# One inference step of a hybrid decoder on one core: sample chain between dense matmuls, gate sums normed earlier, parked sums added later

## The chip, the core and the metric

The kernel runs on one core of a Trainium2 chip. Its engines are TensorE (PE: matmuls; PEld: its weight loads), VectorE (DVE), ScalarE (ACT), GpSimd (POOL) and SyncE (SP). SP only issues transfers; ACT and POOL issue some beside their other work. The metric is the time of one execution on the device in microseconds, as the median of several runs. A profiled execution gives a trace with the start, length and releaser of every instruction.

## The reference

One layer for 512 prompt tokens and for 8 sequences of 4 sample tokens, in float32:

```python
h = h + 0.5 * rmsnorm(swiglu(rmsnorm(h, norm_g[0]), wg[0], wu[0], wd[0]), norm_g[1])
m, c_kv, k_r, s_fin = mixer(rmsnorm(h, norm_g[2]), ...)
h = h + rmsnorm(m, norm_g[3])
h = h + 0.5 * rmsnorm(swiglu(rmsnorm(h, norm_g[4]), wg[1], wu[1], wd[1]), norm_g[5])
def swiglu(x, wg, wu, wd):
    return (jax.nn.silu(x @ wg) * (x @ wu)) @ wd
```

The width is 1024, the inner width of both FFNs 2816. The mixer has four heads of a gated linear recurrence (HGRN2) and four heads of latent attention; the sample tokens attend to 4096 cached positions, which lie in pages of 128 rows and are found through a page table. Eight results are returned, the two token outputs, new cache rows and the recurrent states.

## The kernel before, in words

All activations lie transposed: the model width on the partitions (8 tiles of 128), the 544 tokens along the free axis. `prompt[0]` and `prompt[1]` are two halves of 256 prompt tokens, and `TP:` are the 32 sample columns, so a half with its share of sample columns, `even[x]`, is W2 = 272 wide. A matmul in float32 precision is made of three of reduced precision: `split` casts a high part on ScalarE (L158, L195, L219) and takes the rest on VectorE (L159, L196, L220), and the products high-high, low-high and high-low are added in one accumulator.

The stages follow one another on TensorE: the first FFN (`ffn0`), the mixer's projections and recurrence, the attention of the prompt, the decode of the sample, the sample chain, the second FFN (`ffn1`) and its end.

*Projection.* `project(x)` computes the attention output of half x times w_o: 8 columns `d`, each from a 512 KB load `wraw<-w_o` (L218), a cast (L219), a subtraction (L220) and 24 matmuls (L246). `weight` gives each column one of NW = 2 pairs of buffers `wh` and `wl`. Behind each column stand a copy (L680), a square (L267) and a scaling (L270) on ScalarE. The old activations `h[x]` of both halves are loaded (L671) into the same tile `q0`, so the load of half 1 comes after half 0 is done with it. `squares(0)` then squares the eight tiles of half 0 at once (L708), and `root` makes the norm of it.

*Decode.* `decode()` yields once per step of a tick. POOL gathers pages, VectorE turns 32x32 blocks (L1379), TensorE takes scores (L1391) and values (L1424), ScalarE and VectorE do the softmax between. `phase_a()` is a second generator, `gb`: project(1), then the gate, up and down columns of the first FA = 8 tiles of the second FFN. Its matmuls over 512 columns are the filler of the decode. The loop at L1604 decides how many filler steps follow one tick: `PRE` for the first ten ticks, one afterwards. `decode_new()` computes the scores of the four new tokens of each sequence and goes with the early odd ticks.

*Sample chain.* `decode_end()` merges the decode's parts, projects them by w_o for the 32 sample columns (`rowprod`, L1492, into `sr`), turns the result (`back`, L1498, into `tp`), and takes two column sums over partitions (`colsum`, L1507, into `pr`: eight matmuls with a matrix of ones per sum). Each sum gives a norm (`rstd`, L185). Only then can the sample columns of the second FFN's input be split, since `ffn1` takes 272 columns at a time with sample columns among them. After each yield of this chain two filler steps are taken, as long as there are some.

*Second FFN.* `ffn1` goes through pairs of tiles j = 4 to 10; j = 4 by `classic`, the others by `seven`, a seven-product scheme with banks X, Y, Z (L447). In each j, `tile_pair` with w_g makes G, then with w_u makes V; `gated(H, *late, i)` of the j before stands in between and multiplies G by the norm r4 (L526), takes the sigmoid (L289 to L291: exponential, plus one, reciprocal) and multiplies (L528, L529). In `seven`, L478 to L484 prepare the weight sums, and `plus` (L496) reads a bank so that it comes free. `fill` puts down-projection matmuls (L228, into `dn`) between the products, `PACE` of them at a time, from the list `downs`. The sums of down projections lie parked in DRAM: mA[0] and mA[1] from the decode's filler, mA[2] from `park` in j = 6. At j = 7 the first two are fetched into mT (L1738: a plain copy by SP, then an accumulating transfer by POOL), at j = 8 all of `downs` is done at once and mA[2] is added by two accumulating transfers (L1743).

*The end.* `lastdown` multiplies the last six tiles by w_d and adds the result to mT, output tiles 0 and 1 first, then 2, then 3 to 7; `Finish` norms and writes.

Within an engine's queue the program order is what the builder makes of the order of the code: `tc.issue_after(mark[0])` lets an instruction stand behind a marked one, and a tile of a pool with N buffers makes the writer wait for the readers of the tile N before.

## Time and profile before

| what | us |
|---|---|
| median of 3 runs (1255.78 to 1258.1) | 1257.3 |
| the profiled execution | 1267.38 |
| its span, first to last instruction | 1265.6 |
| TensorE busy | 1223.2 (97%) |
| VectorE busy | 981.6 (78%) |
| ScalarE busy | 703.3 (56%) |
| POOL busy | 91.2 (7%) |
| mean granted TensorE clock | 0.988 |

Times in the trace are counted from the start of the span. The first FFN lies before about 375, the mixer up to 575, the prompt's attention up to 701, project(1) between 701 and 730, the decode up to about 974, the sample chain from 974 to 994, `ffn1` up to about 1225. In a row of the timeline the bracket at the end tells how long the engine stood idle before the instruction, and what ended it. In a row of equal windows, the busy times are given with the number of instructions behind them. L numbers are lines of the kernel before.

### The profile page before, as it was taken

How to read it: one execution, taken by the hardware profiler on the slowest of the kernel's cores; microseconds unless marked ns; L12 is line 12 of the kernel's file. 1: busy time of each engine (PE TensorE's matmuls, PEld its weight loads, DVE VectorE, ACT ScalarE, POOL GpSimd, SP SyncE). 2: the span in 40 equal slices, each digit the busy share in tenths (PEclk: the TensorE clock that was granted, in tenths of full speed). 3: DMA queues.
4: the chain of work that ended last, by engine and by line, in shares of the span. 5: the costliest groups of instructions: out<-in, count | busy, mean ns of one | idle time of the engine just before them, and what ended most of it. 6: DMA issues, size and time to landing. Idle time of an engine off the chain costs nothing.

```text
span 1265.6 us, 29473 instructions
## 1 busy us (share of the span) xinstructions
PE 1223.2 (97%) x12244; PEld 1122.7 (89%) x12244; DVE 981.6 (78%) x1992; ACT 703.3 (56%) x1524; POOL 91.2 (7%) x102
## 2 busy tenths in 40 slices
PE   8999999999999999999999899999999999999997
PEld 7999999999999988989989777667677999999997
DVE  7897778888678887777886778878885759768765
ACT  7675545454566644545677655545455346554363
POOL 0000000000000000000000212332321000000000
PEclk9999999999999999999999899999999899999999
DMA  6233323332165221333325765688568467764231
GB/s 234 84 117 100 99 86 100 101 100 80 52 224 165 67 87 65 92 88 128 114 73 150 268 235 191 218 300 304 201 233 294 148 256 239 172 180 119 80 109 71
DMA packets 82070, 190.70 MB, mean 151 GB/s; under 512 B 14032, under 2 KB 39664, under 8 KB 77456
## 3 DMA queue, kind: packets, MB, share of 16 engines
q1 hardware_dynamic: 60208, 117.60, 28.7%
q0 software_dynamic: 15840, 63.58, 15.5%
q10 hardware_dynamic: 5888, 7.65, 1.8%
q8 instruction: 96, 1.57, 0.5%
q14 instruction: 38, 0.31, 0.1%
HBM read 172.63 MB, written 16.16 MB: 149 GB/s over the span
## 4 chain that ended last, share of the span: by engine, by line
PE 79%; DVE 10%; ACT 5%; DMA 4%; issue 2%; SPq 0%; DVEq 0%; ACTq 0%
PE acc L246 19%; PE acc L228 11%; PE dn L228 10%; PE Y L447 8%; PE Z L447 6%; PE X L447 5%; PE s L1391 3%; PE acc L627 3%; PE acc L1800 2%; PE o L1424 2%; DVE kh L1379 1%; DMA wraw<-w_u 1%; PE pa L957 1%; DMA wraw<-w_g 1%; ACT pbuf L1415 1%
## 5 line engine op out<-in xcount | busy, mean ns | idle before, releaser
L246 PE MATMUL acc<-uh,wh 128*128 128x272 f32 (+2 forms) x496 | 161.1, 325 | 0.7 <-ACT uh L195 0.7
L246 PE MATMUL acc<-ul,wh 128*128 128x272 f32 (+2 forms) x496 | 155.7, 315 | 0.7 <-DVE ul L196 0.7
L246 PE MATMUL acc<-uh,wl 128*128 128x272 f32 (+2 forms) x496 | 155.3, 314 | 0.5 <-DVE wl L220 0.5
L220 DVE TENSOR_TENSOR wl<-wraw,wh 128x1024 fp32r<-128x1024 f32 (+2 forms) x80 | 86.2, 1078 | 35.8 <-ACT wh L219 33.4
L219 ACT CAST wh<-wraw 128x1024 fp32r<-128x1024 f32 (+2 forms) x80 | 74.8, 935 | 67.1 <-PE acc L246 49.3
L228 PE MATMUL dn<-hh,dh 128*128 128x272 f32 x384 | 111.4, 290 | 0.0
L228 PE MATMUL dn<-hh,dl 128*128 128x272 f32 x384 | 110.5, 288 | 0.0
L228 PE MATMUL dn<-hl,dh 128*128 128x272 f32 x384 | 110.5, 288 | 0.0
L246 PEld LDWEIGHTS acc<-uh,wh 128*128 128x128 f32 x496 | 93.2, 188 | 14.1 <-issue 9.1
L246 PEld LDWEIGHTS acc<-uh,wl 128*128 128x128 f32 x496 | 93.1, 188 | 7.0 <-issue 1.3
L246 PEld LDWEIGHTS acc<-ul,wh 128*128 128x128 f32 x496 | 93.3, 188 | 6.2 <-issue 1.2
L228 PEld LDWEIGHTS dn<-hh,dh 128*128 128x128 f32 x384 | 72.3, 188 | 1.0 <-issue 0.2
L228 PEld LDWEIGHTS dn<-hl,dh 128*128 128x128 f32 x384 | 72.5, 189 | 0.0
L228 PEld LDWEIGHTS dn<-hh,dl 128*128 128x128 f32 x384 | 72.1, 188 | 0.0
L158 ACT CAST sh<-wraw 128x512 fp32r<-128x512 f32 (+1 forms) x66 | 40.7, 657 | 44.3 <-PE Z L447 27.3
L158 ACT CAST wh<-wraw 128x512 fp32r<-128x512 f32 (+1 forms) x67 | 41.0, 651 | 39.9 <-PE Z L447 22.5
L1391 PEld LDWEIGHTS s<-kh,q 64*32 64x32 f32 x2560 | 38.6, 105 | 26.5 <-issue 19.1
L1391 PE MATMUL s<-kh,q 64*32 64x128 f32 x2560 | 54.3, 273 | 7.6 <-issue 5.6
L158 ACT CAST dh<-wraw 128x512 fp32r<-128x512 f32 x48 | 29.8, 620 | 48.0 <-PE dn L228 43.6
L159 DVE TENSOR_TENSOR wl<-wraw,wh 128x512 fp32r<-128x512 f32 (+1 forms) x67 | 46.8, 726 | 7.8 <-ACT wh L158 7.2
L1415 ACT COPY pbuf<-pt 32x64 f32<-32x64 f32 x192 | 46.5, 242 | 9.3 <-DVE pt L1411 6.6
L159 DVE TENSOR_TENSOR sl<-wraw,sh 128x512 fp32r<-128x512 f32 (+1 forms) x66 | 46.6, 734 | 3.8 <-ACT sh L158 3.0
(708 smaller groups left out, 4131.1 us busy)
## 6 DMA issues: line engine op xcount, KB each, us to landing
wraw<-w_u SPq DMA_DIRECT2D x44, 512.0 KB
wraw<-w_g SPq DMA_DIRECT2D x43, 512.0 KB
wraw<-w_d SPq DMA_DIRECT2D x24, 512.0 KB
wraw<-w_in SPq DMA_DIRECT2D x24, 512.0 KB
wraw<-w_o SPq DMA_DIRECT2D x16, 512.0 KB
wraw<-w_d SPq DMA_DIRECT2D x16, 384.0 KB
wraw<-w_d SPq DMA_DIRECT2D x16, 256.0 KB
mA<-sit ACTq DMA_DIRECT2D x16, 256.0 KB
```

The source lines that it names most:

```text
L158: nc.scalar.copy(hi, src)
L159: (eng or nc.vector).tensor_tensor(lo, src, f32(hi), op=ALU.subtract)
L219: nc.scalar.copy(wh[:, :kt], w[:, :kt])
L220: nc.vector.tensor_tensor(wl[:, :kt], w[:, :kt], f32(wh[:, :kt]), op=ALU.subtract)
L228: nc.tensor.matmul(out, a, b, start=n == 0, stop=n == last)
L246: nc.tensor.matmul(acc[:, :n], a[:, k], b[:, k], start=k + i == 0, stop=k == kt - 1 and i == 2)
L447: nc.tensor.matmul(bank, a[p][:, k], b[q][:, k], start=first and k + n == 0, stop=k == 3 and n == 2, skip_group_check=True)
L627: nc.tensor.matmul(accs[x, d], wts[d][p][:, k], hs[k // 2][q][:, k % 2, x], start=k + n == 0, stop=k == nf - 1 and n == 2)
L1391: nc.tensor.matmul(self.s[r][c * 32 : c * 32 + 32, :P], q[rs, j], kh, start=st + jj == 0, stop=st == len(JS) - 1 and jj == 1, skip_group_c ...
L1415: (nc.scalar.copy if g else nc.vector.tensor_copy)(self.p[g * 32 : g * 32 + 32, c // 2, c % 2 * 4 : c % 2 * 4 + 4, self.i * 16 : self.i * ...
L1424: nc.tensor.matmul(o[g : g + 32, :R], self.p[:, c, a], self.craw[c][:, a], start=i + c == 0 and a < 4, stop=i + c == 2 and a >= 4, skip_gr ...
L1800: nc.tensor.matmul(accs[x, d], wts[d][p][:, k], hs[k // 2][q][:, k % 2, x], start=k + n == 0, stop=k == nf - 1 and n == 2)
```

## The change

It has five parts.

1. **project(1).** Its `h[1]` gets a slot of its own (`m`), so that the load goes out earlier. `weight` takes a ready pair of buffers by `home`, and every third column of project(1) gets such a pair, called `hl`. `squares` becomes a generator, of which one square follows each step of project(1); `root(0, ..)` comes at step 9 in place of 2. `sil` has one buffer in place of two.
2. **Decode.** `decode_new` starts after tick 12 and has its temporaries in other tiles. The gather slots are in another order, and the third and fourth gather are placed otherwise. The filler goes by `PRE, BODY = 22, 95`: 22 steps over the first 14 ticks, 73 over the next 80. Before it was 22 over 10, and one for each tick after.
3. **Sample chain.** It moves out of `decode_end` into `sample_u`. `decode_end` has 3, 4 and 1 filler steps behind its yields, `sample_u` two behind each. `colsum` is one matmul over 256 columns and a reduction on VectorE. The pools of `ffn1` open before it, and the first weights of w_g are split before it.
4. **Gate sums.** G is multiplied by r4 right after the products that make it, in place of at the head of `gated`, an iteration later.
5. **Parked sums.** `settle(d)` adds four of the eight output tiles of mA[2]: `settle(0)` at j = 10, `settle(4)` after the last `fill`. The `fill(99)` at j = 8 is gone, and all fetches at j = 7 are issued by POOL.

ScalarE, in j = 5 of `ffn1`: `sit` is the sigmoid, `ha` a pair of gate sums, `dh` the high part of a w_d tile for the down projection, `hb<-X` the reader of bank X. Before:

```order
L499 COPY tq<-X 128x272
L289 ACTIVATE sit<-ha 128x544
L290 ACTIVATE sit<-sit,ones 128x544
L158 CAST dh<-wraw 128x512
L291 ACTIVATE sit<-sit 128x544
L158 CAST dh<-wraw 128x512
L505 COPY hb<-X 128x272
```

and now (lines of the changed kernel, where the sigmoid's three are L288 to L290 and the reader of X is L504):

```order
L498 COPY tq<-X 128x272
L288 ACTIVATE sit<-ha 128x544
L289 ACTIVATE sit<-sit,ones 128x544
L290 ACTIVATE sit<-sit 128x544
L158 CAST wh<-S 128x512
L504 COPY hb<-X 128x272
L158 CAST wh<-S 128x512
L158 CAST dh<-wraw 128x512
L158 CAST hh<-ha 128x544
L158 CAST dh<-wraw 128x512
```

Both casts `dh` moved behind the third step of the sigmoid.

TensorE, in the sample chain from the turning of the projected rows (`tp`) to the second column sum (`pr`), before; `acc` are the first products of `ffn1`:

```order
L1498 MATMUL tp<-ident,rs_t 128x128 x2
L1507 MATMUL pr<-s_post,ones 128x32 x8
L228 MATMUL acc<-uh,sh 128x272
L228 MATMUL acc<-ul,sh 128x272
L228 MATMUL acc<-uh,wh 128x272
L1507 MATMUL pr<-s_post,ones 128x32 x8
```

and now, around the first of the two sums, where L1331 is the column sum and the rows L245 are filler:

```order
L245 MATMUL acc<-hh,wh 128x512
L245 MATMUL acc<-hl,wh 128x512
L245 MATMUL acc<-hh,wl 128x512
L1331 MATMUL pr<-s_post,ones 128x256
L245 MATMUL acc<-hh,wh 128x512
L245 MATMUL acc<-hl,wh 128x512
```

Twelve filler matmuls now stand ahead of each step of this chain and twelve more behind the first sum; the second sum stands behind 14 of the products of `ffn1`.

ScalarE, in project(1): the w_o columns are cast in the rows `wh<-wraw` (before) and `hl<-wraw` (the third pair). Before:

```order
L680 COPY hh<-acc 128x256 x2
L267 ACTIVATE ssq<-hh 128x256
L219 CAST wh<-wraw 128x1024
L708 ACTIVATE sq_8792<-q_8242 128x256
L708 ACTIVATE sq_8795<-q_8242 128x256
```

and now, with line numbers of the changed kernel:

```order
L683 COPY hh<-acc 128x256 x2
L266 ACTIVATE ssq<-hh 128x256
L266 ACTIVATE sq_8856<-hh 128x256
L269 ACTIVATE hh<-hh,gv 128x256 x2
L711 ACTIVATE sq_8860<-q_8242 128x256
L218 CAST hl<-wraw 128x1024
```

The cast moved behind a second square, the two scalings and a square of half 0.

The diff, without the unchanged functions that it moves ahead of the decode:

```diff
-PRE = (2, 2, 2, 2, 2, 2, 2, 2, 3, 3)
+PRE, BODY = 22, 95
...
-    def weight(srcs, kt, staged=False):
+    def weight(srcs, kt, staged=False, home=None):
         pool, sfx, bufs = (st, "x", STAG) if staged else (sb, "", NW)
         w = mk([P, 8, P], F32, "wraw", 5, pool=sb)
-        wh = mk([P, 8, P], F32R, "wh" + sfx, bufs, pool=pool)
-        wl = mk([P, 8, P], F32R, "wl" + sfx, bufs, pool=pool)
+        wh, wl = home or [mk([P, 8, P], F32R, n + sfx, bufs, pool=pool) for n in ("wh", "wl")]
...
-    def block_ffn(i, B, r=None):
+    def block_ffn(i, B):
...
         def gated(H, G, V, i):
             z = G[:, 2 * i : 2 * i + 2]
             t = mk([P, 2, W2], F32, "sit", 2)
-            if r is not None:
-                nc.vector.tensor_tensor(z, z, r, op=ALU.mult)
             sigmoid(t, z)
...
     def project(x, o, nxt, pool=None):
-        if not qts:
+        if x:
+            h[x] = actslot("m", 1, n=HS[0])
+        else:
             qts.append(mk([P, 2 * KQ * HS[0]], F32, "q0", pool=dK))
-        h[x] = qts[0][:, : KD * HS[0]].rearrange("p (k t) -> p k t", k=KD)
+            h[x] = qts[0][:, : KD * HS[0]].rearrange("p (k t) -> p k t", k=KD)
         nc.sync.dma_start(h[x], hsp[:, :, prompt[x]])
         yield
         mT = mk([P, KD, HS[0]], F32, "hh", pool=pool) if pool else actslot("m", x, n=HS[0])
         sacc = tmp("ssq", HS[0])
 
         def wo(d):
-            return weight([wcols(w_o, 0, KD, d * P)], KD)
+            home = None
+            if pool and d % 3 == 2:
+                home = mk([P, 2, KD, P], F32R, "hl", pool=pool)
+                home = home[:, 0], home[:, 1]
+            return weight([wcols(w_o, 0, KD, d * P)], KD, home=home)
...
             nc.scalar.activation(q, h[x][:, k], AF.Square)
             if k:
                 nc.vector.tensor_tensor(acc, acc, q, op=ALU.add)
-        return acc
+            yield acc
...
-        acc = squares(0)
         pj = project(1, oo[1], to_ffn, ffa)
         next(pj)
+        sq = squares(0)
         for n, _ in enumerate(pj):
-            if n == 2:
+            acc = next(sq, None) or acc
+            if n == 9:
                 root(0, acc)
...
+    def colsum(q):
+        pr = ps("pr", PRT)[:, : KD * TS]
+        nc.tensor.matmul(pr, ones, q.rearrange("p k t -> p (k t)"), start=True, stop=True)
+        t = mk([P, TS], F32, "tS", 1, pool=sb)
+        nc.vector.tensor_reduce(t, pr.rearrange("p (k t) -> p t k", k=KD), axis=AX.X, op=ALU.add)
+        return t
...
+    def sample_u():
+        hS = srow("ssq")
+        nc.sync.dma_start(hS, hsp[:, :, TP:])
+        tok = tmp("rs_t", 2 * P)
+        for r in range(2):
+            nc.scalar.copy(tok[:, r * P : (r + 1) * P], rowprod(oTs, wo[r]))
+            yield
+        tp = back(tok)
+        yield
+        mS, sq = srow("ssq"), srow("s_post")
+        nc.scalar.activation(sq, tp, AF.Square)
+        nc.vector.tensor_tensor(mS, tp, gains(3), op=ALU.mult)
+        s = mk([P, TS], F32, "sS", 1, pool=sb)
+        rstd(s, colsum(sq), D)
+        yield
+        nc.vector.tensor_tensor(mS, mS, over(s), op=ALU.mult)
+        nc.vector.tensor_tensor(hS, hS, mS, op=ALU.add)
+        nc.sync.dma_start(hs2[:, :, TP:], hS)
+        sq = srow("s_post")
+        nc.scalar.activation(sq, hS, AF.Square)
+        uS, uR = srow("sq1"), srow("sq1")
+        nc.vector.tensor_tensor(uS, hS, gains(4), op=ALU.mult)
+        split(u4[0][:, :, TP:], u4[1][:, :, TP:], uS)
+        rstd(u4[2][:, TP:], colsum(sq), D)
+        nc.vector.tensor_tensor(uR, uS, over(u4[2][:, TP:]), op=ALU.mult)
+        smp.extend((uS, uR))
...
-        slots = ("ma", "dx0", "dx1", "mb", "ha", "hb", "q0")
+        slots = ("ma", "dx0", "dx1", "q0", "ha", "hb", "mb")
...
-                    if n < 3 and st == 0:
+                    if n < 2 and st == 0:
                         if n == 0:
                             H[0].gather_r()
-                        gather(2 + n // 2)
+                        gather(2)
+                    if n == 2 and st == 3:
+                        gather(3)
...
-        def colsum(q):
-            pr = ps("pr", PRT)[:, :TS]
-            for k in range(KD):
-                nc.tensor.matmul(pr, ones, q[:, k], start=k == 0, stop=k == KD - 1)
-            return pr
...
         ga, gn = decode(), decode_new()
+        ib = 0
         for ia in range(len(JS) * (NH2 + 2) + 4):
             next(ga)
-            if ia % 2:
+            if ia % 2 and ia > 12:
                 next(gn, None)
-            for _ in range(PRE[ia] if ia < len(PRE) else 1):
+            while ib < PRE and ib * 14 < (ia + 1) * PRE or ib >= PRE and (ib - PRE) * 80 < (ia - 13) * (BODY - PRE):
                 next(gb)
+                ib += 1
         for _ in ga:
             pass
-        for _ in decode_end():
-            for _ in range(2):
+        for n, _ in enumerate(decode_end()):
+            for _ in range((3, 4, 1)[n]):
                 next(gb, None)
 
+    sst = ExitStack()
+    side[0] = sst.enter_context(tc.tile_pool(name="str2", bufs=1, side="right", reuse_waits="tile"))
+    spin[0] = 1
+    ws = [[wsplit(w) for w in raw_pair(w_g[1], FA)]]
+    for _ in sample_u():
+        for _ in range(2):
+            next(gb, None)
     for _ in gb:
         pass
     dks.close()
...
-                ws = [wsplit(w) for w in raw_pair(src, 2 * j)]
+                w = ws.pop() if ws else [wsplit(w) for w in raw_pair(src, 2 * j)]
                 for x in BOTH:
-                    classic(ws, C, x, ucol)
+                    classic(w, C, x, ucol)
                     next(sc, None)
                 if mid:
                     mid()
             else:
                 seven(raw_pair(src, 2 * j), C, mid)
                 next(sc, None)
+
+        def settle(d):
+            for x in BOTH:
+                nc.gpsimd.dma_start(mT[x][:, d : d + 4], mA[2][:, d : d + 4, even[x]], accum_op=ALU.add)
...
-                        (nc.gpsimd.dma_start if i else nc.sync.dma_start)(mT[x][:, :, :n], mA[i][:, :, even[x].start : even[x].start + n], **({"accum_op": ALU.add} if i else {}))
-            if j == 8:
-                fill(99)
-                owed[0] = 0
-                for x in BOTH:
-                    nc.gpsimd.dma_start(mT[x], mA[2][:, :, even[x]], accum_op=ALU.add)
+                        nc.gpsimd.dma_start(mT[x][:, :, :n], mA[i][:, :, even[x].start : even[x].start + n], **({"accum_op": ALU.add} if i else {}))
+            if j == 10:
+                settle(0)
             tile_pair(j, w_g[1], G)
+            for i in range(2):
+                nc.vector.tensor_tensor(G[:, 2 * i : 2 * i + 2], G[:, 2 * i : 2 * i + 2], r4v, op=ALU.mult)
...
         fill(99)
+        settle(4)
```

## The prediction

> **What bounds the kernel now.** I read the page's head first, then the windows of equal length, then the idle gaps of TensorE one by one, and last the queues of the engines that end those gaps.

> ```profile
> span 1265.6 us, 29473 instructions
> PE 1223.2 (97%) x12244; PEld 1122.7 (89%) x12244; DVE 981.6 (78%) x1992; ACT 703.3 (56%) x1524; POOL 91.2 (7%) x102
> PE 79%; DVE 10%; ACT 5%; DMA 4%; issue 2%; SPq 0%; DVEq 0%; ACTq 0%
> ```

> TensorE is busy for 97% of the span and carries 79% of the chain that ended last. No other engine comes near. So only two things can be won: the 42 us in which TensorE is idle, and the stretches in which it is busy but slow. The change removes almost no matmul. The windows around the places that it touches (columns: stretch, its length, busy time of PE, PEld, DVE, ACT, POOL with instruction counts, granted TensorE clock, DMA share, GB/s):

> ```profile
> 700.00:705.00 5.00, 2.53 (x18) 2.06 (x17) 5.00 (x14) 3.83 (x10) 2.04 (x3) 0.87 0.44 147
> 705.00:710.00 5.00, 4.10 (x18) 3.80 (x19) 5.00 (x10) 3.19 (x9) 4.29 (x3) 0.50 1.02 344
> 710.00:715.00 5.00, 5.00 (x40) 4.95 (x39) 2.37 (x4) 3.62 (x9) 0.06 (x1) 0.94 1.02 419
> 715.00:720.00 5.00, 3.16 (x28) 2.88 (x26) 4.34 (x8) 4.28 (x8) 0.00 (x0) 1.00 1.04 372
> 720.00:725.00 5.00, 5.00 (x29) 5.00 (x30) 2.57 (x6) 0.78 (x1) 0.00 (x0) 0.66 0.98 374
> 980.00:985.00 5.00, 2.91 (x20) 2.61 (x20) 3.46 (x7) 2.19 (x5) 0.55 (x1) 0.86 0.71 218
> 985.00:990.00 5.00, 5.00 (x24) 4.86 (x24) 2.66 (x6) 1.87 (x5) 0.00 (x0) 0.50 0.49 135
> 990.00:995.00 5.00, 5.00 (x28) 5.00 (x27) 5.00 (x5) 0.00 (x0) 0.00 (x0) 0.61 0.00 0
> 1135.00:1140.00 5.00, 2.65 (x22) 2.43 (x20) 2.06 (x5) 3.85 (x8) 0.88 (x1) 1.00 0.52 146
> 1140.00:1145.00 5.00, 4.91 (x27) 4.91 (x28) 4.26 (x9) 0.85 (x2) 0.56 (x1) 0.66 0.81 127
> ```

> The clock column is the second loss. One minus the clock, times the row's length, is the time lost: 0.65 + 2.50 + 0.30 = 3.45 us at 700 to 715, 1.70 at 720, 0.70 + 2.50 + 1.95 = 5.15 at 980 to 995, and 1.70 at 1140. Each time the clock fell in or right behind a row in which TensorE had been busy for 3.16 us of 5 or less. The smallest step is 1.70 us, so I take that as the price of one drop.

> The idle gaps themselves stand in the timeline (in brackets, the gap and what ended it):

> ```profile
> 704.79 0.77 PE L1331 MATMUL b<-ident,q 128*128 128x128 f32 x2 [2.00 <-DVE mxs L1322]
> 706.89 0.58 PE L246 MATMUL acc<-ha,wl 128*128 128x256 f32 x1 [0.90 <-issue]
> 719.98 0.39 PE L246 MATMUL acc<-ha,wl 128*128 128x256 f32 x1 [1.84 <-DVE wl L220]
> 1046.04 0.39 PE L447 MATMUL Y<-uh,wh 128*128 128x272 f32 x1 [2.76 <-DVE hb L496]
> ```

> **First part: project(1).** Its activations get a slot of their own, so their load is issued ahead of the w_o columns; the squares of half 0 are spread, and every third weight gets a third pair of hi/lo buffers. The second gap, 1.84 us with its 1.70 us of clock, ends when wl (the low half of a w_o column) is made; with a third pair the split of that column needs no longer wait for the matmuls of the one before it. I count it as gone: −3.5. The first gap (2.00 + 0.90, with 3.45 of clock) I leave. Moving decode_new away takes L1331 out of that place, but the next matmul there needs a wl too, and in ScalarE's new order that column's cast stands behind one more L267, two L270 and a square, four instructions of this kind:

> ```profile
> 705.43 0.51 ACT L270 ACTIVATE hh<-hh,gv 128x256 f32<-128x256 f32 x1
> ```

> That is up to 2.0 us later, on an engine that was busy for 3.83 us of the first 5. The load that moves is 1 MB on SP's queue, now ahead of the w_o columns; at the 372 to 419 GB/s of the rows 710 to 720 it could hold them up by 2.7 us, unless it is issued while the queue is still idle (share 0.44 in 700 to 705). Bounds: both gaps and their clock gone, −9.9; neither gone and the columns later, +2.7.

> **Second part: decode earlier, with less filler.** In the decode stage the generator of dense columns gives TensorE something to do between the score and value matmuls. One step of it is two groups of three 128x512 matmuls:

> ```profile
> 970.96 0.39 PE L246 MATMUL acc<-hh,wl 128*128 128x512 f32 x1
> 973.75 0.40 PE L246 MATMUL acc<-hh,wl 128*128 128x512 f32 x1
> 750.00:775.00 25.00, 24.04 (x505) 17.48 (x499) 21.69 (x45) 11.78 (x30) 5.67 (x6) 1.00 0.48 161
> 900.00:925.00 25.00, 24.17 (x450) 17.66 (x449) 21.99 (x48) 11.29 (x32) 7.59 (x8) 1.00 0.67 224
> ```

> From the first to the second of these rows there are 12 matmuls in 2.79 us, 0.2325 each, so a step is 1.40 us. Before, 22 steps went with the first 10 ticks and 84 with the other 84. Now 22 go with 14 ticks and 73 with 80. Eleven steps, 15.3 us, leave the decode. They are not saved; they are done in the sample chain, where I book what they replace. What counts here is whether decode gets shorter by those 15.3 us. VectorE is busy for about 22 us of 25; decode's roughly 215 us would become 200, and VectorE's share of it rises from 0.88 to 0.94. That still fits, with less slack: I take +2 for stalls that the filler covered. Bounds: 0, and +15.3 if VectorE or the gathers already set the pace, so that the filler only used waiting time. The value is near the low end because TensorE, with 24.0 to 24.2 us of 25, is the fuller engine. The rest of the move (decode_new later, its temporaries in other slots, the scores earlier) I cost at 0: the same instructions, under the same dense columns.

> **Third part: the sample chain.** It runs from 973.99 to 993.9 and ends when ffn1 is at full clock.

> ```profile
> 980.00:994.00 14.00, 11.91 (x60) 11.47 (x61) 10.12 (x15) 4.05 (x9) 0.55 (x1) 0.63 0.43 126
> L1507 PE MATMUL pr<-s_post,ones 128*128 128x32 f32 x32 | 5.6, 340 | 0.5 <-ACT s_post L1563 0.5
> L228 PE MATMUL acc<-uh,sh 128*128 128x272 f32 x6 | 2.7, 445 | 1.6 <-ACT sh L158 1.6
> L1531 PE MATMUL pb<-q,ones x2: 379/431/483, 965.7 to 966.1; 128*128 128x256 f32 x2
> 1046.27 0.29 PE L447 MATMUL Y<-ul,wh 128*128 128x272 f32 x1
> 1047.52 0.29 PE L447 MATMUL Y<-uh,wl 128*128 128x272 f32 x1
> ```

> The last 14 us hold 60 matmuls: two transposes, 32 of the column sum L1507, and 26 of 128x272. At full clock ten of the latter take 1.25 us (the last two rows and the nine between), so 26 take 3.25. The new column sum is one fp32 matmul over 256 columns; L1531 has that shape, as two pieces from 965.7 to 966.1 and 0.48 more, so about 0.7 us, and two of them are 1.4. With 0.3 for the transposes that is 4.95 us of work in 14, and 9.0 us to be had: 2.1 idle (0.5 + 1.6), 5.15 clock and the shorter sums. The change puts twelve 128x512 matmuls (2.8 us) between every two steps of the chain; the gaps it has to cover were 0.5 and 1.6. I take −9. The other bound is −3: if the filler ends up in the wrong place and the clock falls again, only the shorter sums and the earlier first sh remain.

> **Fourth part: gate sums normed at once, parked sums late.** The gap at 1046.04 has this behind it on ScalarE and VectorE:

> ```profile
> 1042.46 0.62 ACT L158 CAST dh<-wraw 128x512 fp32r<-128x512 f32 x1 [3.43 <-DMA wraw<-w_d]
> 1042.99 0.65 ACT L291 ACTIVATE sit<-sit 128x544 f32<-128x544 f32 x1
> 1043.67 0.72 DVE L528 TENSOR_TENSOR ha<-ha,sit 128x544 f32<-128x544 f32 x1 [3.12 <-ACT sit L291]
> 1045.55 0.43 DVE L496 TENSOR_TENSOR hb<-Y,tq 128x272 f32<-128x272 f32 x1
> ```

> A cast of w_d that waits for its transfer stands ahead of the last step of the sigmoid; the gate product waits for that, and the bank's reader L496 for the gate product. In the new order both dh casts of that place stand behind the sigmoid: −2.75. The other two gaps are in the second row below (total, times, longest; three gaps of 2.76, 1.74 and 2.44):

> ```profile
> PE Y L447 <- DVE hb L496: 6.9, 3, 2.8
> 1095.28 0.69 DVE L478 TENSOR_TENSOR S<-wraw 128x512 f32<-128x512 f32 x1 [5.02 <-DMA wraw<-w_g]
> 1100.80 0.72 DVE L526 TENSOR_TENSOR ha<-ha,rn 128x544 f32<-128x544 f32 x1
> 1138.99 0.69 DVE L478 TENSOR_TENSOR S<-wraw 128x512 f32<-128x512 f32 x1 [2.94 <-DMA wraw<-w_u]
> 1075.00:1100.00 25.00, 25.00 (x201) 25.00 (x201) 15.81 (x28) 14.11 (x29) 1.46 (x1) 1.00 0.91 195
> mb<-mA POOLq DMA_DIRECT2D x1, 960.0 KB, 10.6
> 1205.00:1210.00 5.00, 5.00 (x42) 5.00 (x42) 3.79 (x7) 4.97 (x10) 0.00 (x0) 1.00 0.00 0
> ```

> Both begin with VectorE waiting for a weight, 5.02 and 2.94 us, while the accumulating transfers of the parked sums share the DMA engines (share 0.91 in 1075 to 1100). The change takes two multiplies (0.72 each) from ahead of L496 at the second gap, and moves the transfers of the third parked sum from iteration 8 to iteration 10 and the end, where the share is as low as 0.00. The last of them moves half of what took 10.6 us for 960 KB, and it is first read by the adds of output tiles 4 and up, after tiles 0 to 3 of the last down projection; I cost it at 0, and at up to 5.3 us if that cover is short. So the third gap and its clock go, −2.44 − 1.70, and the second, −1.74. Against that, the first two parked sums still move in iteration 7, now all on POOL's queue, behind which only the later sums stand, while SP's weight loads no longer queue behind two of them; and the burst of down matmuls at iteration 8, which covered the late w_g, is gone, because its work is spread. If w_g is still 5.02 us late there, no burst hides it. I book +2.6, half of that wait, between 0 and 5.02. The part as a whole: −2.75 − 1.74 − 4.14 + 2.6 = −6.0, bounds −8.6 and, if both waits of 5.02 and 2.94 come through whole and only 1046 is repaired, +3.

> **The sum:** −3.5 + 2 − 9 − 6 = −16.5. On the profiled execution (span 1265.6, run 1267.4) that is a span of 1249. The median of the runs is 1257.3, 10.1 below that execution, and I carry the difference over unchanged: 1240.8, rounded to **1240 us**.

> [...] In the trace the clock halved after gaps of 1.84 and 2.44 us. [...]

> **The rivals.** First, the drops of the clock do not hang on these gaps. For it: 1046.04 had the longest gap, 2.76, and no drop behind it. Against it: all four drops stand behind the four emptiest rows. Then 1.70 + 5.15 + 1.70 of the sum return, 8.5 us, and the time is about 1249; chance 0.08.

> Second, the transfers stay the bound in ffn1: the copies on POOL and the weights collide once more, and the fourth part gives nothing. For it: the DMA share of 0.91. Against it: 0.00 at 1205. The time is 1247; chance 0.20.

> Third, decode is paced by VectorE. For it: 22 us of 25. Against it: TensorE's 24. The second part then costs 15.3 instead of 2: 1254; chance 0.12.

> Fourth, slower than before: with less filler, TensorE falls below the density at which the clock stays full, in the decode. Each drop costs 1.70, and there are some sixteen halves of about 13 us. From 10 drops on the whole gain of 16.5 is gone; one in each half costs 27 and gives 1267. For it: thinning was enough at 980. Against it: in 750 to 775 and 900 to 925 the clock is 1.00 with 1 us idle, and a half loses only 0.9 us of filler in 13. Chance 0.07.

> **How the numbers follow.** The forecast has 0.53. Its own range: with all lower bounds together 1240 − 6.4 − 2 − 2.6 = 1229; with one part at its upper bound (first +6.2, third +6, fourth +9) up to 1249. The range that holds 8 in 10 takes in the second and most of the third rival: 1229 to 1254. A difference under 0.2%, 2.5 us, cannot be told from none. Faster by more takes the forecast, the first two rivals and the half of the third that lies below 1254.8: 0.87. Within 0.2%: 0.06. Slower: 0.07, the fourth.

> **What would show it.** Right: no gap over 1 us at the sums of the sample chain and a clock of 1.00 from there into ffn1; no wait of Y L447 for hb over 1 us; at the first w_o columns one drop left, at the third none. The second part is right if decode ends some 13 us earlier against its start. Wrong: score matmuls that wait for kh more than the 0.8 us they do now at most, or a clock below 1.00 between 750 and 960; a wait for w_g or w_u over 3 us on VectorE with TensorE idle behind it; lastdown waiting for mT.

## The result, and the profile after

The changed kernel takes 1246.4 us (median of 5 runs, 1245.2 to 1248.2) against 1256.6 us of the kernel before (5 runs). The ratio is 0.9923, with a 95% interval of 0.9906 to 0.9940: 0.8% faster. The forecast was 1240 in a range of 1229 to 1254, and faster with 0.87. The direction and the range hold; the gain is 10 us in place of 17.

The head of the page of the changed kernel:

```profile
span 1244.6 us, 29432 instructions
PE 1210.0 (97%) x12216; PEld 1114.2 (90%) x12216; DVE 981.5 (79%) x1994; ACT 702.8 (56%) x1524; POOL 93.1 (7%) x106
```

TensorE still bounds the kernel. The two profiled spans lie 21.0 us apart, twice what the medians say. So the first question was whether the profile that the forecast was read from is a usual execution of the kernel before. The kernel before was profiled once more (e1 below), and its span was 1252.2. In it, the last products of the first two w_o columns (the earlier ones stand among those of the attention), a product of the first gate column just behind the column sum that ends project(1), the first matmul `o` of the sample chain and the first sample row of the second FFN start here:

```profile
701.27 0.50 PE L257 MATMUL acc<-ha,wh 128*128 128x256 f32 x2 [0.46 <-ACT ha L158]
729.72 0.47 PE L246 MATMUL acc<-ul,wh 128*128 128x256 f32 x1
960.52 1.21 PE L1553 MATMUL o<-q,kh 128*128 128x32 f32 x10
983.29 0.30 PE L1492 MATMUL sr<-ma,sq 128*32 128x128 f32 x2
```

and in the changed kernel here:

```profile
700.16 0.50 PE L256 MATMUL acc<-ha,wh 128*128 128x256 f32 x2 [0.46 <-ACT ha L158]
733.33 0.47 PE L245 MATMUL acc<-ul,wh 128*128 128x256 f32 x1
954.50 1.20 PE L1611 MATMUL o<-q,kh 128*128 128x32 f32 x10
984.56 0.30 PE L1317 MATMUL sr<-ma,sq 128*32 128x128 f32 x2
```

Differences of these starts, and of the ends of the spans, give the time by stage. The last column is what the forecast's terms say for the same stage (the filler that it moved, 15.3 us, leaves the decode and enters the chain):

| stage | before, again | after | measured | forecast |
|---|---|---|---|---|
| ahead of project(1) | 701.27 | 700.16 | −1.1 | 0 |
| project(1) | 28.45 | 33.17 | +4.7 | −3.5 |
| decode | 230.80 | 221.17 | −9.6 | −15.3 + 2 |
| sample chain | 22.77 | 30.06 | +7.3 | +15.3 − 9 |
| ffn1 and end | 268.91 | 260.04 | −8.9 | −6 |
| sum | 1252.2 | 1244.6 | −7.6 | −16.5 |

Most of the gain comes from the second FFN. Decode and chain together gain 2.3 us, and project(1) loses 4.7; against the first profile of the kernel before, where it took 31.50, it loses 1.7. The sum is 2.6 us less than the 10.2 of the medians: the execution of e1 (1254.0) lies that much below the median of before (1256.6), while that of the changed kernel is its median.

What the losses look like in the changed kernel: two gaps of TensorE in project(1), one in the chain (timeline).

```profile
704.95 0.58 PE L245 MATMUL acc<-ha,hl 128*128 128x256 f32 x1 [3.28 <-ACT hl L218]
709.80 0.80 PE L245 MATMUL acc<-ha,hl 128*128 128x256 f32 x2 [4.06 <-DVE hl L219]
978.13 0.70 PE L1331 MATMUL pr<-s_post,ones 128*128 128x256 f32 x2 [2.56 <-ACT s_post L1364]
```

and the granted clock around them (equal windows; the value behind the last count in brackets is the clock):

```profile
700.00:705.00 5.00, 1.28 (x7) 0.88 (x7) 2.88 (x7) 5.00 (x14) 4.12 (x4) 0.74 0.64 201
705.00:710.00 5.00, 0.94 (x3) 0.65 (x4) 3.00 (x5) 2.10 (x3) 3.58 (x4) 0.50 0.98 334
710.00:715.00 5.00, 5.00 (x24) 5.00 (x25) 5.00 (x8) 0.10 (x1) 0.58 (x1) 0.50 1.00 419
715.00:720.00 5.00, 5.00 (x40) 5.00 (x39) 3.29 (x6) 4.31 (x10) 0.00 (x0) 0.90 1.01 407
975.00:980.00 5.00, 2.44 (x14) 2.17 (x13) 1.73 (x4) 1.86 (x5) 0.00 (x0) 0.88 1.01 328
980.00:985.00 5.00, 5.00 (x45) 4.85 (x47) 5.00 (x5) 0.72 (x2) 0.00 (x0) 0.77 0.02 9
```

By one minus the clock, project(1) loses 1.30 + 2.50 + 2.50 + 0.50 = 6.8 us to the clock, where the kernel before loses 3.45 + 1.70 in the first profile and 3.40 in e1 (0.89, 0.50 and 0.93 in the same first three rows). The chain loses 0.60 + 1.15 = 1.75, where the first profile of before loses 5.15. What stands behind the second and the third gap is told by the queues. VectorE, ahead of the low half `hl` of the third w_o column:

```profile
707.00 0.71 DVE L1476 STREAM_TRANSPOSE kh<-rraw 128x512 f32<-128x512 f32 x1 [3.68 <-DMA rraw<-pool_r,idx]
708.57 1.18 DVE L219 TENSOR_TENSOR hl<-wraw,hl 128x1024 fp32r<-128x1024 f32 x1
```

A block turn of the decode waits 3.68 us for its gather, and the low half waits behind it. In the kernel before a turn stands ahead of a low half too, but it does not wait, because its gather goes out almost 25 us sooner; in e1:

```profile
676.25 1.01 POOL L1371 DMA_INDIRECT rraw<-pool_r,idx  x1 [0.16 <-issue]
704.31 0.70 DVE L1379 STREAM_TRANSPOSE kh<-rraw 128x512 f32<-128x512 f32 x1
```

and in the changed kernel:

```profile
699.76 0.95 POOL L1444 MEMSET pbuf<- 128x1024 f32 x1 [57.38 <-PE o L1247]
700.89 1.47 POOL L1468 DMA_INDIRECT rraw<-pool_r,idx  x1 [0.18 <-DVE hb L159]
```

On POOL the gather stands behind the clearing of a buffer of the decode (`pbuf`), and this now starts only when a product of the prompt's attention (L1247) has ended. It starts between 699.8 and 700.8 in every profile of a kernel with the change, and at 675.1 and 675.4 in the two of the kernel before. Which line of the change moved it was not tried.

ScalarE, ahead of the square for the second column sum:

```profile
977.18 0.59 ACT L755 COPY sit<-acc 128x512 f32<-128x512 f32 x1 [2.52 <-DMA mA<-sit]
977.66 0.42 ACT L1364 ACTIVATE s_post<-ssq 128x256 f32<-128x256 f32 x1
```

A copy that parks a column of the filler waits 2.52 us for the transfer that still reads its tile (two tiles are shared by all such copies), and the square waits behind it. In the second FFN the three waits of a Y product are gone; the list of waits of TensorE from 1000 on is, for the kernel before again,

```profile
PE Y L447 <- DVE hb L496: 6.6, 3, 2.6
```

and for the changed kernel

```profile
PE dn L227 <- DVE hb L495: 0.2, 1, 0.2
PE pr L1646 <- ACT sq L266: 0.2, 1, 0.2
```

6.6 us of waits and one drop of the clock (1.7) make 8.3 of the 8.9 us.

### The profile page after: what moved, and what is told of

Same layout as the page of the kernel before. It is cut to its first block, busy times and chain, and to the rows that moved or that the text cites. A ratio compares the mean times of both kernels' runs of the same rounds, so it can differ in the third digit from the quotient of the medians.

```text
span 1244.6 us, 29432 instructions
## 1 busy us (share of the span) xinstructions
PE 1210.0 (97%) x12216; PEld 1114.2 (90%) x12216; DVE 981.5 (79%) x1994; ACT 702.8 (56%) x1524; POOL 93.1 (7%) x106
## 4 chain that ended last, share of the span: by engine, by line
PE 80%; DVE 7%; issue 6%; DMA 4%; ACT 3%; POOL 0%; DVEq 0%; SPq 0%; POOLq 0%
PE acc L245 19%; PE dn L227 12%; PE Y L446 9%; PE acc L227 9%; PE Z L446 6%; PE X L446 6%; PE acc L1821 3%; PE acc L624 3%; PE s L1488 3%; PE o L1521 2%; DMA ma<-w_g 1%; DVE kh L1476 1%; PE pa L962 1%; PE s L1215 1%; DMA wraw<-w_u 1%
## 5 line engine op out<-in xcount | busy, mean ns | idle before, releaser
L245 PE MATMUL acc<-uh,wh 128*128 128x272 f32 (+2 forms) x496 | 161.7, 326 | 0.5 <-ACT uh L195 0.5
L245 PE MATMUL acc<-ul,wh 128*128 128x272 f32 (+2 forms) x496 | 156.6, 316 | 0.9 <-DVE ul L196 0.9
L245 PE MATMUL acc<-uh,wl 128*128 128x272 f32 (+2 forms) x496 | 155.7, 314 | 0.0
L219 DVE TENSOR_TENSOR wl<-wraw,wh 128x1024 fp32r<-128x1024 f32 (+2 forms) x78 | 83.8, 1075 | 37.0 <-ACT wh L218 36.7
L245 PEld LDWEIGHTS acc<-uh,wh 128*128 128x128 f32 x496 | 93.3, 188 | 15.1 <-issue 9.9
L245 PEld LDWEIGHTS acc<-ul,wh 128*128 128x128 f32 x496 | 93.4, 188 | 7.1 <-issue 1.6
L245 PEld LDWEIGHTS acc<-uh,wl 128*128 128x128 f32 x496 | 93.3, 188 | 6.1 <-issue 1.1
L158 ACT CAST wh<-wraw 128x512 fp32r<-128x512 f32 (+1 forms) x67 | 41.0, 651 | 40.3 <-PE Z L446 22.6
L158 ACT CAST sh<-wraw 128x512 fp32r<-128x512 f32 (+1 forms) x66 | 40.6, 657 | 38.4 <-PE Z L446 26.0
L158 ACT CAST dh<-wraw 128x512 fp32r<-128x512 f32 x48 | 29.8, 621 | 45.5 <-PE dn L227 44.2
L1488 PE MATMUL s<-kh,q 64*32 64x128 f32 x2560 | 49.5, 273 | 2.3 <-issue 2.3
```

The lines of the kernel that those rows point to most:

```text
L158: nc.scalar.copy(hi, src)
L219: nc.vector.tensor_tensor(wl[:, :kt], w[:, :kt], f32(wh[:, :kt]), op=ALU.subtract)
L245: nc.tensor.matmul(acc[:, :n], a[:, k], b[:, k], start=k + i == 0, stop=k == kt - 1 and i == 2)
L1488: nc.tensor.matmul(self.s[r][c * 32 : c * 32 + 32, :P], q[rs, j], kh, start=st + jj == 0, stop=st == len(JS) - 1 and jj == 1, skip_group_c ...
```

## The experiments

Times of runs are compared through their ratio to the kernel before on the same chip, since the chips differ: the kernel before took 1255.2 us where e1 to e4 ran, 1265.4 where e5 to e8 ran, and 1256.1 where e9 to e12 ran. Stages differ between executions too: project(1) took 31.7 to 34.1 us in the eight profiles that have it as the change makes it (the first of the changed kernel, e5 to e8 and e10 to e12).

**e1: the kernel before again.** No edit.

> The kernel before, unchanged. Its profiled execution was 1267.4 us, 10.8 above the median of its runs (1256.6), while the profiled execution of the changed kernel, 1246.4, is its median. Theory A: the profiled execution of before was an unusual one, with stalls that most of its runs do not have; then a new profile gives a span of about 1254 to 1258, the mean clock is above 0.988, and some of the gaps at 719.98, 1046.04, 1103.80, 1140.09 or the drops of the clock behind them are smaller or missing. Theory B: the profiler itself adds about 10 us to this kernel; then a new profile gives a span near 1265 with the same gaps. In both the ratio of times is 1.000.

Measured: ratio 1.0002 (0.9991 to 1.0013), span 1252.2. Theory A holds, but by only one of the four gaps that it named: the gap of 1.84 us at 719.98 and its drop are not there, while the three waits of the second FFN and the clock's drop in the chain are there again. The span is 13.4 us shorter, of which 3.05 are in project(1) (28.45 in place of 31.50), and 10.1 in the decode, which theory A did not name. The score matmuls of the decode, in the page of the first profile and of this one:

```profile
L1391 PE MATMUL s<-kh,q 64*32 64x128 f32 x2560 | 54.3, 273 | 7.6 <-issue 5.6
```

```profile
L1391 PE MATMUL s<-kh,q 64*32 64x128 f32 x2560 | 47.7, 273 | 4.3 <-DVE kh L1379 2.3
```

Busy and idle together, 61.9 against 52.0 us: 9.9 of the 10.1. The same line took 56.2 to 57.5 us, with 7.1 to 7.4 idle, in e5 to e8, on the chip where the kernel before takes 1265.4, and 47.7 to 50.5 with at most 4.3 idle in all profiles from the other chips and in the changed kernel. The first profile reads like those of the slower chip, but on which chip it was taken is not on record. So this goes with the chip, as far as is known, and not with the change; why these small matmuls are issued more slowly there stays open.

**e2: block turns later on VectorE.** The first turn is put behind the low half of the fourth w_o column, which `low[1]` keeps.

```diff
+                    if top is None and h_.n == 0:
+                        top = low[1]
                     with tc.issue_after(top.ins) if top is not None else nullcontext():
                         h_.turn(st)
```

> The changed kernel, with the decode's first block turns ordered behind the low half of the fourth w_o column on VectorE. Theory A: the new gap of 4.06 us at 709.80 comes from turns that wait for a gather (3.68 us) ahead of the low half on VectorE; then this gap falls below 1.5 us, one or two drops of the clock go with it, and the time falls by 3 to 7 us to about 1241. Rival: the gap comes from the weight's transfer or the cast on ScalarE; then it stays at about 4 us and the time is 1246.

Measured: ratio 0.9927 (0.9910 to 0.9943), no change against 0.9923. The mechanism is as in theory A, the gain is not. The gap fell from 4.06 to 0.47 us, and two others opened behind it:

```profile
707.00 0.79 PE L247 MATMUL acc<-ha,hl 128*128 128x256 f32 x2 [0.47 <-DVE hl L221]
719.80 0.51 PE L247 MATMUL acc<-ha,hl 128*128 128x256 f32 x2 [2.05 <-DVE hl L221]
725.27 0.70 PE L179 MATMUL pr<-ssq,ones 128*128 128x256 f32 x2 [1.87 <-DVE ssq L718]
```

VectorE's own rows say why: the turns now wait further on, again ahead of a low half.

```profile
712.53 0.71 DVE L1481 STREAM_TRANSPOSE kh<-ma 128x512 f32<-128x512 f32 x1 [1.77 <-DMA ma<-pool_c,idx]
716.66 0.71 DVE L1481 STREAM_TRANSPOSE kh<-dx 128x512 f32<-128x512 f32 x1 [3.42 <-DMA dx<-pool_c,idx]
718.53 1.22 DVE L221 TENSOR_TENSOR hl<-wraw,hl 128x1024 fp32r<-128x1024 f32 x1
```

project(1) took 33.0 us, as before the edit (33.2). Moving one of several waiting turns moves the wait.

**e3: the third column split early.**

```diff
+            first = [wo(d) for d in range(3)]
-            for d, acc in enumerate((yield from gemm_2([wo(d) for d in range(2)], o))):
+            for d, acc in enumerate((yield from gemm_2(first[:2], o))):
                 column(d, acc)
...
-            column(d, (yield from gemm_q(wo(d), o, 4)) if pool else gemm(wo(d), o))
+            column(d, (yield from gemm_q(first[2] if d == 2 else wo(d), o, 4)) if pool else gemm(wo(d), o))
```

> The changed kernel, with the third w_o column's split called ahead of the first two columns' matmuls, so that its cast stands ahead of the copies and squares of these columns on ScalarE. Theory A: the gap of 3.28 us at 704.95 comes from the place of this cast; then it falls to about 1 to 1.5 us, and since the low half now stands ahead of the waiting turns, the gap of 4.06 moves to the next column and is smaller: the time falls by 2 to 6 us. Rival: both gaps are set by the gather that the turns wait for; then one gap is filled and the other grows by as much, and the time stays at 1246.

Measured: ratio 0.9911 (0.9894 to 0.9928), 1244.0 us; project(1) 30.43 in place of 33.17. Theory A: the two gaps became smaller ones, the three largest of which are here.

```profile
702.92 0.58 PE L245 MATMUL acc<-ha,hl 128*128 128x256 f32 x1 [1.03 <-ACT hl L218]
704.19 0.80 PE L245 MATMUL acc<-ha,hl 128*128 128x256 f32 x2 [0.47 <-DVE hl L219]
710.34 0.39 PE L245 MATMUL acc<-ha,wh 128*128 128x256 f32 x1 [1.08 <-ACT wh L218]
```

The third pair of buffers lets the cast be made while TensorE still works on the columns ahead, but only if the cast also stands there in ScalarE's queue (the gap ahead of that column is 1.03 us here and 3.28 in the changed kernel, which has the pair too). The gain by stage is 2.7 us, and 1.3 against the shortest project(1) of the eight above; it is at the edge of what the ratio can tell.

**e4: no third pair of buffers.**

```diff
-            if pool and d % 3 == 2:
+            if False:
```

> The changed kernel without the third pair of hi/lo buffers in project(1); all else is kept. Theory A: the third pair is worth little as it is used, because its cast stands behind the same copies as before; the time stays within 2 us of 1246. Rival: it took away the second stall (1.84 us and a drop of the clock); without it the time rises by 2 to 5 us and a gap ahead of a later column's low half comes back.

Measured: ratio 0.9919 (0.9903 to 0.9936), 1245.8 us. Theory A: as the change uses it, the third pair is worth nothing that can be measured. The same two gaps are there, 3.27 and 4.79 us; project(1) took 34.05.

**e5: a third tile for the parking copies.** In the second half of the filler the tile `sil` is free and serves as the third.

```diff
-                t = mk([P, TP], F32, "sit", 2, pool=ffa)
+                t = mk([P, TP], F32, "sil", 1, pool=ffa) if c and d % 3 == 2 else mk([P, TP], F32, "sit", 2, pool=ffa)
```

> The changed kernel, with a third tile for the copies that park the last down columns of the filler. Theory A: the gap of 2.56 us ahead of the second column sum comes from ScalarE, where a parking copy waits 2.52 us for the transfer that still reads its tile, ahead of the square that the sum needs; with a third tile the gap falls below 0.5 us, the drop of the clock behind it goes, and the time falls by about 4 us (2.56 + 1.70) to 1242. Rival: the sum waits for the row work of the chain on VectorE; then the gap stays near 2 us and the time at 1246.

Measured: ratio 0.9930 (0.9917 to 0.9943). The gap is gone, and so is the drop; the windows of the chain read

```profile
980.00:985.00 5.00, 5.00 (x25) 4.12 (x24) 2.60 (x4) 3.21 (x7) 0.00 (x0) 1.00 0.99 365
985.00:990.00 5.00, 5.00 (x34) 4.57 (x33) 3.54 (x8) 2.85 (x8) 0.00 (x0) 1.00 1.03 369
```

and the chain took 25.94 us, where e6 on the same chip, with the gap, took 28.53. The ratio does not show it: it is that of the changed kernel. On this chip the decode took 233.33 us, 12.2 more than in the first profile of the changed kernel, while the two profiles of the kernel before, of which the first reads like this chip, differ by 10.1 there; so the change may gain some 2 us less on this chip (an estimate from these four decodes). By stage theory A holds. By the whole time this run does not decide, since the changed kernel itself was not run on this chip.

**e6: gate sums multiplied late again.**

```diff
+            if r is not None:
+                nc.vector.tensor_tensor(z, z, r, op=ALU.mult)
             sigmoid(t, z)
...
-            for i in range(2):
-                nc.vector.tensor_tensor(G[:, 2 * i : 2 * i + 2], G[:, 2 * i : 2 * i + 2], r4v, op=ALU.mult)
```

> The changed kernel with the gate sums multiplied by the norm at the head of the gate product again, an iteration later. Theory A: the three waits of a Y product for its bank's reader went because the multiplies moved; then at least the one of 2.76 us comes back and the time rises by 2.5 to 5 us. Rival: they went because the transfers of the parked sums moved; then none or only one of them comes back and the time stays within 1.5 us of 1246.

Measured: ratio 0.9952 (0.9938 to 0.9965). The time rose by 2.8 us against e5 on the same chip, but not for the reason of theory A: by stage the chain took 2.6 us more, the gap that e5 does not have, and project(1), which this edit does not touch, 1.3. The second FFN took 259.78 us, as in the changed kernel (260.04), and none of the three waits came back. Of the move of the multiplies no effect is seen, so the −2.75 that the forecast booked in the same part is not due to it. That e7 brings back only the other two waits leaves the cause of the third to e11.

**e7: parked sums as before.**

```diff
-            if j == 10:
-                settle(0)
+            if j == 8:
+                fill(99)
+                owed[0] = 0
+                for x in BOTH:
+                    nc.gpsimd.dma_start(mT[x], mA[2][:, :, even[x]], accum_op=ALU.add)
...
         fill(99)
-        settle(4)
```

(and the plain copies of iteration 7 by SP).

> The changed kernel with the parked sums as before: the burst of down products and the whole third sum at iteration 8, the plain copies issued by SP. Theory A: the waits of 1.74 and 2.44 us with one drop of the clock come back, since a weight is late behind the accumulating transfers; the time rises by 4 to 6 us to about 1251. Rival (the wait that I booked at 2.6 in the forecast): without the burst the late w_g had nothing to hide it, so bringing it back costs only 2 to 3 us net; about 1248.5.

Measured: ratio 1.0013 (1.0001 to 1.0024), no gain over the kernel before left; the second FFN took 266.26 us, 6.5 more than in e6. Theory A: two of the three waits are back (waits of TensorE from 1000 on),

```profile
PE Y L446 <- DVE hb L495: 3.8, 2, 2.3
```

with one drop of the clock, and on VectorE the two late weights ahead of them:

```profile
1091.26 0.69 DVE L477 TENSOR_TENSOR S<-wraw 128x512 f32<-128x512 f32 x1 [4.65 <-DMA wraw<-w_g]
1135.71 0.69 DVE L477 TENSOR_TENSOR S<-wraw 128x512 f32<-128x512 f32 x1 [2.78 <-DMA wraw<-w_u]
```

This part of the change alone is worth about 6.5 us. The burst, the third sum in one piece at iteration 8 and the copies on SP were put back together; which of the three brings the waits was not tried apart.

**e8: the filler spread as before.**

```diff
-            while ib < PRE and ib * 14 < (ia + 1) * PRE or ib >= PRE and (ib - PRE) * 80 < (ia - 13) * (BODY - PRE):
-                next(gb)
-                ib += 1
+            for _ in range(OLD[ia] if ia < 10 else 1):
+                next(gb)
```

(`OLD` holds eight times 2 and twice 3).

> The changed kernel with the filler of the decode spread as before: 22 steps with the first 10 ticks, then one with each. Fewer steps are then left for the sample chain. Theory A: a filler step is neither saved nor lost in decode, only moved, and what it earns is the idle time and clock that it covers in the chain; then decode gets longer by 1.4 us for each step, the chain gets shorter by less, with gaps and drops of the clock in it, and the time rises by 3 to 6 us. Rival: the decode had waiting time that the filler only used, so that the same steps cost nothing there; then the time stays at 1246 or falls.

Measured: ratio 0.9925 (0.9912 to 0.9938), as the changed kernel; 1255.0 us against 1256.3 for e5 on the same chip. The decode took 243.45 us and the chain 16.26, together 259.7; in e5 they took 233.33 and 25.94, together 259.3, and in e6, which has the two tiles of the changed kernel and its gap, 262.3. So the filler is moved and neither saved nor lost, as theory A says, but the time did not rise by the 3 to 6 us of theory A, because the chain did not need it: with no filler at all its gaps were 0.57 and 0.91 us, and the clock stayed at 1.00. The rival has the time right and not the reason, since the decode did get 10 us longer. What stands in the filler's place is in these rows: the two sums (L1332) stand among products of the second FFN, whose first weights are split early.

```profile
982.04 0.33 PE L1324 MATMUL tp<-ident,rs_t 128*128 128x128 f32 x1
982.85 0.70 PE L1332 MATMUL pr<-s_post,ones 128*128 128x256 f32 x2
987.88 0.70 PE L1332 MATMUL pr<-s_post,ones 128*128 128x256 f32 x2 [0.57 <-ACT s_post L1365]
992.38 0.30 PE L1318 MATMUL sr<-ma,sq 128*32 128x128 f32 x2 [0.91 <-DVE hl L1770]
```

**e9: three edits together.** e2, e3 and e5.

> The changed kernel with three edits together: the third w_o column split ahead of the first two columns' matmuls, the first block turns behind the low half of the fourth, and a third tile for the parking copies. Theory A: the gaps in project(1) and in the chain were each paid by TensorE; then project(1) takes 29 to 30.5 us in place of 33.2, the chain 26 in place of 30, and the kernel is 5 to 8 us faster than the changed one, on the same chip. Rival: what is won at one place is waited for at the next, and it is within 2 us of the changed kernel.

Measured: 1238.7 us, ratio 0.9862 (0.9843 to 0.9881), against 1245.8 for the changed kernel in the same series (e12): 7.1 us faster, and the best kernel here. project(1) took 29.00 us, the chain 25.92. Of the gaps over 1 us from project(1) on, two are left outside the decode, the second with a drop of the clock:

```profile
702.99 0.38 PE L247 MATMUL acc<-ha,hl 128*128 128x256 f32 x1 [1.03 <-ACT hl L220]
718.89 0.91 PE L179 MATMUL pr<-ssq,ones 128*128 128x256 f32 x2 [2.40 <-DVE ssq L719]
```

Theory A holds. project(1) is 1.4 us shorter than with e3 alone, which is less than it differs between executions; so what e2 adds to e3 is not shown.

**e10: no early split of the first w_g weights.**

```diff
-    ws = [[wsplit(w) for w in raw_pair(w_g[1], FA)]]
+    ws = []
```

> The changed kernel without the early split of the first w_g weights: they are split where ffn1 asks for them, as before. Theory A: the chain is shorter than before because products of ffn1 stand ready to fill it, whether or not there is dense filler; without the early split they come late, the chain takes 2 to 5 us more and the clock drops once or twice. Rival: the dense filler is what covers the chain; then the early split is worth nothing and the time is that of the changed kernel.

Measured: ratio 0.9925 (0.9907 to 0.9943), 1245.5 us; the chain took 27.52 us, with a gap of 1.55. The rival: with the filler in the chain the early split is worth nothing. With e8 this says that either cover is enough; both taken away at once was not tried.

**e11: the phase of the weight rings.** The weights of the second FFN are split into two rings of buffers in turn, and one line sets with which it begins.

```diff
-    spin[0] = 1
```

> The changed kernel without the one line that sets the phase of the two weight rings before ffn1. Theory A: this line, and not the earlier multiply, put the casts of w_d behind the sigmoid in iteration 5; without it one wait of a Y product of 2 to 2.8 us comes back there, and the time rises by 1.5 to 4 us. Rival: the wait went because w_d lands earlier than before; then it stays away and the time is that of the changed kernel.

Measured: ratio 0.9934 (0.9916 to 0.9951), 1246.8 us against 1245.8 for e12: the mechanism of theory A, the price hidden in the spread of the runs. In iteration 5 the first cast of w_d stands ahead of the sigmoid's last step again,

```profile
1025.19 0.62 ACT L158 CAST dh<-wraw 128x512 fp32r<-128x512 f32 x1 [3.84 <-DMA wraw<-w_d]
1025.72 0.65 ACT L290 ACTIVATE sit<-sit 128x544 f32<-128x544 f32 x1
```

and the wait of the Y product is back:

```profile
1028.77 0.40 PE L446 MATMUL Y<-uh,wh 128*128 128x272 f32 x1 [3.17 <-DVE hb L495]
```

The second FFN took 263.75 us, 4.3 more than in e12. The same line also changes the order of ScalarE and VectorE in the chain, which was 2.8 us shorter here and had no gap. project(1) was 2.1 us shorter too, but its instructions stand in the same order as in e12, so that is not due to the line. With both, the whole hardly moved.

**e12: the changed kernel again.** No edit.

> The changed kernel, unchanged, beside the three others on the same chip. Theory A: its ratio to the kernel before is the same on any chip, 0.992, whether the kernel before takes 1255 or 1265 us there, since what differs between chips is the time of the decode's score matmuls, which both kernels have. Rival: the change itself took away what is slow on the slower chip; then the ratio is lower where the kernel before is slower, near 0.985.

Measured: ratio 0.9923 (0.9906 to 0.9939), 1245.8 us; by stage 33.77, 220.83, 29.60 and 259.41 us, as in the first profile within 0.7. The kernel before took 1256.1 on this chip, so the two theories are not told apart; how the changed kernel does on the slower chip was not measured.

## Why the prediction was right, and where its steps were wrong

**The baseline.** The sum was made against a profiled execution with two losses that e1 does not have: 10.1 us in the score matmuls, which no term used, and 3.05 us in project(1), which the first term was made of. The distance of 10.1 us between that execution and the median was carried over as a constant. For the score matmuls that did no harm; for project(1) a gain was booked on a stall that only one of two profiles has, and how many of the other runs have it is not known.

**First part, −3.5: wrong in sign, and its stall was misread.** The forecast took the gap of 1.84 us at 719.98 for a wait for buffers, which a third pair would end ("needs no longer wait for the matmuls of the one before it"). The profile that it was read from shows another cause. The high part of that column was ready at 716.2, and its low half stood on VectorE behind four block turns of the decode, the first of which waited for its gather:

```profile
715.66 0.71 DVE L1379 STREAM_TRANSPOSE kh<-dx 128x512 f32<-128x512 f32 x1 [1.70 <-DMA dx<-pool_c,idx]
718.71 1.22 DVE L220 TENSOR_TENSOR wl<-wraw,wh 128x1024 fp32r<-128x1024 f32 x1
```

In e1 the same turn does not wait and the gap is not there; in e4 there is no third pair, and no gap comes back at that place. So the stall was a late gather, and in the changed kernel even the first gather goes out late, almost 25 us later than before. There the second step failed: the rest of the move ("decode_new later, its temporaries in other slots, the scores earlier") was costed at 0 as "the same instructions, under the same dense columns". The instructions are the same, but their gathers go out at another time, and what stands behind the waiting turns was not named. project(1) measured +4.7 against e1, beyond the upper bound of +2.7, and +1.7 against the first profile. That the first gap would stay because of ScalarE's queue was right (2.00 us before, 3.28 after), and e3 shows the cast's place as its cause.

**Second part, +2: right, on a smaller move.** Nine steps, not eleven, were left for the chain: 54 matmuls of 0.2325 us, 12.6 us. The decode got 9.6 shorter, so 2.9 of the 12.6 us did not come off, near the 2 that was booked for the thinner cover. The third and fourth rivals did not come: the clock is 1.00 through the decode in all profiles but one (a single drop in e2), and the decode got shorter by most of the filler that left it, which it would not if VectorE set the pace.

**Third part, −9: mechanism right, size off, and the reason only half right.** 30.06 is 22.77 plus 12.6 minus 5.3. The gap behind the copy's wait on ScalarE and the drop of the clock (2.56 + 1.75) account for the missing 3.7 us; without them e5 has 25.94, which is 12.6 less 9.4. But it is not the filler that earns this: e8 has the same sum of decode and chain without it. What is left to have earned it are the two sums of one matmul and, in e8, the weights that are ready early; neither was undone without the filler, so this is argued and not shown. The filler brought the parking copies into the chain, and with them the wait.

**Fourth part, −6: too small, and one reason wrong.** Measured −8.9: all three waits and one drop went. Two of them hang on the parked sums (e7: the burst, the third sum's transfers and the copies together), and the +2.6 that I booked for a late w_g without the burst did not come, since with the third sum moved w_g is no longer that late (VectorE's longest wait for a weight from 1000 on is 2.5 us, for a w_u). The third wait did not go because of the multiplies (e6), but because the phase of the rings moved the casts (e11). The effect was read rightly from the new order of ScalarE; which line of the diff makes that order, the forecast did not ask.

**The rivals.** None came as told. The first, on the clock, is answered below. The second named 1247, within a microsecond of the result, and its mechanism is still wrong: the fourth part gave 8.9 us and not nothing. The errors by stage, in the order of the table, are −1.1, +8.2, +3.7, +1.0 and −2.9: 8.9 of the 16.5 us were not earned in the profiles. In the medians the gain is 10.2. That the result lies in the range is in part luck, since the fourth part gave more than was booked while the first gave less than nothing.

## What to carry to other kernels

A transfer that goes out later is paid by whoever stands behind the instruction that waits for it (here a gather 24.6 us later, a turn that waited 3.68 us for it and a gap of TensorE of 4.06): when a change moves buffers or stages, compare when the transfers are issued, on the issuing engine too, and look for those that land late under instructions that others stand behind. An idle engine that waits for a product says where to look and not why: the engine that makes the product has a queue of its own, and its rows belong to the reading (the gap of 1.84 us at 719.98 named VectorE, whose queue held a turn that had waited 1.70 us for its gather). Before a sum is made from one profile, its time is to be set against the median of the runs; a profiled execution that is 10 us off has losses that a second profile can name. A change that is made of several edits is best undone edit by edit, by stages between fixed markers: here one edit gave most of the gain, a gather that goes out later gave part of it back, and a one-line phase of a buffer ring did what was read as part of a larger move.

## What the runs showed of the hardware

```profile
975.43:978.85 3.42, 0.86 (x6) 0.67 (x5) 0.49 (x1) 1.31 (x3) 0.00 (x0) 1.00 1.07 325
```

Of all such windows at full clock between 20 and 1225 us, each of the nineteen in which TensorE was busy for less than 1.6 us was followed by a drop (among them two of the first profile of before, with 1.58 us at 717.40 and 0.97 at 1137.24), and none in which it was busy for more than 2.4. Between the two it went either way; the fullest window with a drop behind it is one of e2, in the decode:

```profile
779.51:782.92 3.41, 2.37 (x13) 1.60 (x12) 3.33 (x10) 0.60 (x2) 0.10 (x1) 1.00 0.90 320
```

So equal gaps fare differently by how they lie on this grid. In the first profile of before, the gap of 1.84 us at 719.98 lies in one window, which leaves 1.58 us of busy time, and the clock fell; that of 2.76 at 1046.04 lies in two, which leaves 1.62 and 2.46, and it did not. The windows ahead of a drop were not idle ones: in the two rows above TensorE was busy for 0.86 and 2.37 us, 25% and 69% of the window. Filling a gap gave the clock back where the gap had emptied one window far enough, as in e5 in the chain, and had none to give back where two windows shared the gap, as in e6: of the prediction's reading, that the drops stand behind the gaps, and of its first rival, each holds in part.

The score matmuls, 64 rows by 128 columns with a weight load each, took 9.9 us more for 2560 of them in one execution than in another of the same kernel (61.9 against 52.0 us, busy and idle together). The executions fall in two groups: the slower one is all of one chip (e5 to e8) and the first profile of before, whose chip is not on record.
